# Softmax attention's logits and values as fp32r passes over four heads

## The chip, the core and the metric

The kernel runs on one core of one Trainium2 chip. A core has five engines with their own instruction queues: TensorE (PE in the profile; its weight loads have a row of their own, PEld), VectorE (DVE), ScalarE (ACT), GpSimd (POOL) and SyncE (SP), which here only issues DMAs. Matrix products land in PSUM, eight banks of 128 partitions x 512 f32; everything else lies in SBUF, 128 partitions wide. The metric is the device time of one execution in microseconds, as the median of several runs.

## The reference

One decoder layer in f32: a SwiGLU network, a pair of token mixers side by side, a second SwiGLU network, each behind a modulated RMSNorm, for 256 positions of width 2048. What matters here is the second mixer, sliding-window attention with 32 query heads, 8 key and value heads (four query heads share one) of width 64, blocks of 128 positions and one sink per query head:

```python
def swa_with_sinks(q, k, v, sinks):
    ...
    kb, vb = band(k), band(v)          # the block before, and the own block
    logits = jnp.einsum('bnqhgd,bnkhd->bnhgqk', qb, kb).astype(jnp.float32) * (d ** -0.5)
    ...
    logits = jnp.where(valid[None, :, None, None], logits, NEG_INF)
    sink = ...
    probs = jax.nn.softmax(jnp.concatenate([logits, sink], axis=-1), axis=-1)[..., :-1]
    out = jnp.einsum('bnhgqk,bnkhd->bnqhgd', probs.astype(v.dtype), vb)
    return out.reshape(b, s, hq * d)
```

With 256 positions there are two blocks (t = 0 and 1 below). The first block sees its own 128 keys, the second its own and those of the first.

## The kernel before, in words

Every large product (`products`, L322 to L324) is made of three fp32r passes. The weight and the activation are each split into a rounded part, `hi`, cast by ScalarE, and the rest, `lo`, which VectorE gets by subtraction; hi*hi, hi*lo and lo*hi are added in PSUM. A projection of 512 output columns, here called a chunk, takes 96 such passes into two PSUM banks (`pa`, four in all, so that chunk n+2 needs the banks of chunk n emptied). The weight is loaded in quarters of a chunk (`load`, L307), each split in two halves (`wh` by L330, `wl` by L331) into a pool of three.

The token mixers' stage runs the chunks of one projection: keys and values of the softmax attention, four chunks of its queries, two of the retention's queries (called rq here) and two of its keys (rk), four of its values (rv), then gates. The attention's own work runs beside the later chunks: `window(pair)` is a Python generator for two query heads, and `step()` takes one piece of it after each quarter chunk. VectorE has further side work in this stage, a matrix-vector product for the conditioning (L203).

For a pair of heads, `window_weights` makes the logits with plain f32 matmuls (L959 for the first block, L962 for the second). The transposed keys `skt` exist twice, with the other half of the partitions zeroed, so that 128 partitions of two query heads can be multiplied with either. Then come scale and mask (L965), maximum (L975, L976), exponential (L996), sum and scaling (L1005), all in one pair tile `a` (a pool of two). `window_values` transposes the weights (L440 into `pd`, a pool of two banks), copies them out (L441 into `t`, a pool of five tiles of 128 x 512) and makes f32 matmuls with the values (L1024, L1028, L1031), whose result is copied into `qo` (L1034). A query chunk is copied out of PSUM into two `t` tiles (L1053) and transposed into `qo`; an rq or rk chunk goes through the rotary (L1074, L1080, L1085, L1086), also with `t` tiles, two for each bank.

The order of SyncE's queue is the program's. Those of PE, VectorE and ScalarE come from a scheduler that, when the program is built, follows the program's order but lets an instruction whose operands and buffers are ready pass one that waits. Once built, every engine's order is fixed.

Of the kernel before, what the change touches and what calls it, by code (L numbers as in the profile page):

```python
# [16 lines left out]
P = 128  # L17
# [25 lines left out]
def constants():  # L43
# [12 lines left out]
    for h in range(RH):  # L56
# [8 lines left out]
                sin.transpose(1, 0, 2).reshape(P, -1),  # L65
                causal,
                before,
# [9 lines left out]
def layer_kernel(  # L77
# [822 lines left out]
    dec = one.tile([P, D], F32, tag="row", name="dec")  # L900
    nc.gpsimd.dma_start(dec, consts[:, C_DEC:])
# [12 lines left out]
    for t in range(NT):  # L914
        nc.gpsimd.dma_start(x_d[:, t, :], x_sb[:, t, :])
    skt = one.tile([P, NT, D], F32, tag="x", name="skt").rearrange(
        "p i (h s) -> p i h s", h=KVH
    )
    VW = HD + KVH * P
    b = in_chunk(O_SV, ready)  # L920
    for t in range(NT):
        for g in range(2):
            kd = t512()
            nc.vector.tensor_copy(
                kd.rearrange("p (h a d) -> p h a d", h=4, a=2),
                head[t][:, g * 256 : (g + 1) * 256]
                .rearrange("p (h d) -> p h d", h=4)[:, :, None, :]
                .broadcast_to([P, 4, 2, HD]),
            )
            ps = bank()  # L930
            for j in range(4):
                js = slice(j * P, (j + 1) * P)
                nc.tensor.transpose(ps[:, js], kd[:, js], ident)
            for i in range(2):
                hs = slice(i * HD, (i + 1) * HD)
                nc.any.tensor_copy(
                    skt[hs, i, g * 4 : g * 4 + 4, t * P : (t + 1) * P],
                    ps[hs].rearrange("p (h s) -> p h s", h=4),
                )
    nc.vector.memset(skt[HD:, 0], 0.0)  # L940
    nc.vector.memset(skt[:HD, 1], 0.0)
    sv = slot()[:, : NT * VW].rearrange("p (t n) -> p t n", t=NT)
    nc.vector.memset(sv, 0.0)
    for t in range(NT):
        nc.any.tensor_copy(
            sv[:, t, HD:].rearrange("p (h d) -> p h d", h=KVH)[:, :, :HD],
            b[t].rearrange("p (h d) -> p h d", h=KVH),
        )
    qo = slot().rearrange("p (k s) -> p k s", s=S)

    mask = small_c[:, C_MASK : C_MASK + 3 * P]

    def window_weights(pair):

        kv = pair // 2
        lg = pair_tile()[:, :, : 3 * P]
        for i in range(2):
            ps = side_bank()
            nc.tensor.matmul(  # L959
                ps[:, :P], qo[:, pair, :P], skt[:, i, kv, :P], start=True, stop=True  # L960
            )
            nc.tensor.matmul(  # L962
                ps[:, P : 3 * P], qo[:, pair, P:], skt[:, i, kv, :], start=True, stop=True
            )
# [7 lines left out]
            )  # L972
        mx = small(4, "mx")
        m2 = mx.rearrange("p (t i) -> p t i", t=2)
        nc.vector.tensor_reduce(out=m2[:, 0, :], in_=lg[:, :, :P], axis=AX.X, op=ALU.max)  # L975
        nc.vector.tensor_reduce(out=m2[:, 1, :], in_=lg[:, :, P:], axis=AX.X, op=ALU.max)  # L976
        sb = sink_b[:, 2 * pair : 2 * pair + 2]
# [14 lines left out]
        for t in range(2):  # L992
            for i in range(2):
                seg = lg[:, i, :P] if t == 0 else lg[:, i, P:]
# [6 lines left out]
        for t in range(2):  # L1001
            for i in range(2):
                seg = lg[:, i, :P] if t == 0 else lg[:, i, P:]
# [4 lines left out]
        return lg  # L1008

    def window_values(pair, lg):  # L1010

        kv = pair // 2
        prs = []
        for i in range(2):
            pr = a512()
            transpose_to(
                pr[:, : 3 * P], lambda j: lg[:, i, j * P : (j + 1) * P], 3, side_bank()
            )
            prs.append(pr)
        po = side_bank()  # L1020
        for i, pr in enumerate(prs):
            vs = slice(kv * P + (1 - i) * HD, kv * P + (1 - i) * HD + P)
            first, last = i == 0, i == 1
            nc.tensor.matmul(po[:, :P], sv[:, 0, vs], pr[:, :P], start=first, stop=last)  # L1024
        for i, pr in enumerate(prs):
            vs = slice(kv * P + (1 - i) * HD, kv * P + (1 - i) * HD + P)
            first, last = i == 0, i == 1
            nc.tensor.matmul(  # L1028
                po[:, P:S], sv[:, 0, vs], pr[:, P : 2 * P], start=first, stop=False
            )  # L1030
            nc.tensor.matmul(  # L1031
                po[:, P:S], sv[:, 1, vs], pr[:, 2 * P : 3 * P], start=False, stop=last
            )
        nc.any.tensor_copy(qo[:, pair, :], po[:, :S])  # L1034

    before = []

    def window(pair):
        lg = window_weights(pair)
        yield  # L1040
        if before:
            window_values(*before.pop())
        before.append((pair, lg))
        if pair == QH // 2 - 1:
            yield
            window_values(*before.pop())
        yield

    for ci in range(4):
        b = in_chunk(O_SQ + ci * CH)  # L1050
        for t in range(NT):
            u = t512()
            nc.any.tensor_copy(u, b[t])  # L1053
            transpose_to(
                qo[:, ci * 4 : ci * 4 + 4, t * P : (t + 1) * P],
                lambda j: u[:, j * P : (j + 1) * P],
                4,
            )
        side += [window(pair) for pair in range(ci * 4, ci * 4 + 4)]
# [33 lines left out]

    vo = slot().rearrange("p (t n) -> p t n", t=NT)
# [194 lines left out]
```

## Time and profile before

| | |
|---|---|
| median of 3 runs | 2455.85 us (2454.01 to 2459.7) |
| the profiled execution's own time | 2457.51 us |
| its span | 2455.7 us |
| PE busy | 2410.4 us, 98% |
| DVE busy | 1706.5 us, 69% |
| ACT busy | 1192.9 us, 49% |
| mean granted PE clock | 0.996 |

The span runs from the first to the last instruction; what the execution takes beside it is 1.8 us. Busy time is the time in which an engine has at least one instruction under way. A recorded duration includes the way out of the engine's pipeline, during which the next instruction may already run; so what an instruction takes from its engine is read from one start to the next, and how late its result is from its duration. In a group's row the columns are line, engine, operation, tiles out<-in, shapes and count, then busy time, mean duration in ns, and the engine's idle time before them with what ended it.

### The profile page before, as it was taken

The numbers are of one execution on the slowest core, as the hardware profiler recorded it, in microseconds if no ns is written. First come the engines' busy times: TensorE is split into PE (matmuls) and PEld (weight loads), VectorE is DVE, ScalarE is ACT, GpSimd is POOL, SyncE is SP. The second block draws the span as 40 slices with busy tenths as digits, with TensorE's granted clock in tenths as the row PEclk, the third lists the DMA queues.
The fourth block names the chain that finished last, engine by engine and source line by source line (L and its number), as shares of the span: only waits on it lengthen the run. The fifth ranks groups of instructions, "written<-read, shape, count | busy, mean of one in ns | idle before, by whom it ended". The sixth has DMA issues, their size and how long they took to land.

```text
span 2455.7 us, 29144 instructions
## 1 busy us (share of the span) xinstructions
PE 2410.4 (98%) x10910; PEld 1985.3 (81%) x10910; DVE 1706.5 (69%) x2731; ACT 1192.9 (49%) x1623; POOL 7.7 (0%) x18
## 2 busy tenths in 40 slices
PE   7999999999999999999999999999999999999998
PEld 5778888887787888888888788887888888888886
DVE  7898877777877677886666776767655555545656
ACT  6544544444546554455544454446544444444544
POOL 0000000000000000000000000000000000000000
PEclk9999999999999999999999999999999999999999
DMA  9997687888876665556676777855566666665563
GB/s 357 340 332 271 234 313 296 326 303 297 311 254 228 231 228 195 205 190 239 230 278 240 258 260 257 276 188 187 206 223 234 228 223 225 238 223 192 188 202 120
DMA packets 244657, 603.27 MB, mean 246 GB/s; under 512 B 9698, under 2 KB 10082, under 8 KB 225186
## 3 DMA queue, kind: packets, MB, share of 16 engines
q1 hardware_dynamic: 243010, 591.61, 67.8%
q0 software_dynamic: 1504, 9.81, 1.0%
q8 instruction: 85, 1.39, 0.2%
q14 instruction: 58, 0.47, 0.1%
HBM read 597.16 MB, written 4.22 MB: 245 GB/s over the span
## 4 chain that ended last, share of the span: by engine, by line
PE 89%; DVE 4%; DMA 1%; ACT 1%; issue 1%; SPq 0%; DVEq 0%; ACTq 0%
PE pa L324 28%; PE pa L323 28%; PE pa L322 28%; PE ps L440 1%; DVE wl L331 1%; DVE slot L203 1%; DMA slot<-in_w_ada_dram 1%; PE pd L962 1%; PE pd L440 0%; DVE home L429 0%; DVE slot L863 0%; PE pd L1024 0%; PE pd L1028 0%; PE pd L1031 0%; PE pd L959 0%
## 5 line engine op out<-in xcount | busy, mean ns | idle before, releaser
L331 DVE TENSOR_TENSOR wl<-raw,wh 128x1024 fp32r<-128x1024 f32 (+1 forms) x788 | 947.6, 1207 | 582.0 <-ACT wh L330 580.2
L330 ACT CAST wh<-raw 128x1024 fp32r<-128x1024 f32 (+1 forms) x788 | 819.5, 1041 | 1043.7 <-PE pa L323 1021.4
L322 PE MATMUL pa<-wh,hh 128*128 128x512 f32 x2200 | 862.4, 393 | 2.2 <-ACT wh L330 1.7
L323 PE MATMUL pa<-wh,hl 128*128 128x512 f32 x2200 | 861.8, 392 | 1.8 <-DVE hl L500 1.8
L324 PE MATMUL pa<-wl,hh 128*128 128x512 f32 x2200 | 796.8, 393 | 2.3 <-DVE wl L331 2.2
L322 PEld LDWEIGHTS pa<-wh,hh 128*128 128x128 f32 x2200 | 413.4, 188 | 89.4 <-ACT wh L330 2.4
L323 PEld LDWEIGHTS pa<-wh,hl 128*128 128x128 f32 x2200 | 413.8, 188 | 87.8 <-DVE hl L500 2.5
L324 PEld LDWEIGHTS pa<-wl,hh 128*128 128x128 f32 x2200 | 410.9, 188 | 89.4 <-DVE wl L331 6.5
L323 PE MATMUL pa<-wh,a 128*128 128x512 f32 x992 | 384.3, 390 | 1.3 <-DVE a L363 1.3
L324 PE MATMUL pa<-wl,a 128*128 128x512 f32 x992 | 368.1, 391 | 1.3 <-DVE wl L331 1.3
L322 PE MATMUL pa<-wh,a 128*128 128x512 f32 x992 | 367.7, 391 | 1.0 <-ACT wh L330 0.5
L324 PEld LDWEIGHTS pa<-wl,a 128*128 128x128 f32 x992 | 185.9, 188 | 42.4 <-DVE wl L331 4.1
L322 PEld LDWEIGHTS pa<-wh,a 128*128 128x128 f32 x992 | 186.6, 188 | 41.4 <-DVE t L552 1.4
L323 PEld LDWEIGHTS pa<-wh,a 128*128 128x128 f32 x992 | 186.5, 188 | 40.3 <-DVE a L363 1.7
L203 DVE CUSTOM_DVE_ANT_0 slot<-slot,cact 128x512 f32<-128x512 f32 (+1 forms) x252 | 192.9, 815 | 28.7 <-DMA slot<-in_w_ada_dram 28.2
L203 DVE CUSTOM_DVE_ANT_0 raw<-raw,cact 128x512 f32<-128x512 f32 (+1 forms) x260 | 166.7, 696 | 43.2 <-DMA raw<-in_w_ada_dram 33.7
L363 DVE TENSOR_TENSOR a<-slot,a 128x512 fp32r<-128x512 f32 x124 | 84.9, 685 | 3.8 <-ACT a L362 3.8
L362 ACT CAST a<-slot 128x512 fp32r<-128x512 f32 x124 | 76.4, 618 | 5.3 <-PE pa L324 5.2
L441 ACT COPY slot<-ps 128x512 f32<-128x512 f32 x76 | 42.4, 586 | 34.8 <-PE ps L440 34.3
L429 DVE TENSOR_TENSOR wl<-raw,wh 128x1024 fp32r<-128x1024 f32 x34 | 41.4, 1223 | 17.4 <-ACT wh L426 17.1
L426 ACT CAST wh<-raw 128x1024 fp32r<-128x1024 f32 x34 | 35.3, 1050 | 17.4 <-PE pa L323 17.3
L203 DVE DVE_READ_ACCUMULATOR2_ANT sums<- 128x1 f32 x512 | 42.5, 83 | 0.0
(171 smaller groups left out, 1174.2 us busy)
## 6 DMA issues: line engine op xcount, KB each, us to landing
raw<-in_w_ffn_gu_dram SPq DMA_DIRECT2D x152, 1024.0 KB, 4.9
raw<-in_w_in_dram SPq DMA_DIRECT2D x104, 1024.0 KB, 5.0
raw<-in_w_ffn_down_dram SPq DMA_DIRECT2D x88, 1024.0 KB, 5.2
slot<-in_w_ada_dram SPq DMA_DIRECT2D x76, 1024.0 KB, 7.6
raw<-in_w_ada_dram SPq DMA_DIRECT2D x64, 1024.0 KB, 4.9
raw<-in_w_ffn_gu_dram SPq DMA_DIRECT2D x24, 768.0 KB, 7.0
raw<-in_w_swa_branch_dram SPq DMA_DIRECT2D x16, 1024.0 KB, 5.2
raw<-in_w_ret_branch_dram SPq DMA_DIRECT2D x16, 1024.0 KB, 5.3
```

The costliest lines, as they stand in the source:

```text
L203: nc.vector.tensor_tensor_reduce(out=w[:, at], in0=w[:, at], in1=cact[:, at], scale=1.0, scalar=0.0, op0=ALU.mult, op1=ALU.add, accum_out= ...
L322: nc.tensor.matmul(ps, ah[:, j, ts], wh[:, j, :], start=first, stop=False)
L323: nc.tensor.matmul(ps, al[:, j, ts], wh[:, j, :], start=False, stop=False)
L324: nc.tensor.matmul(ps, ah[:, j, ts], wl[:, j, :], start=False, stop=last)
L330: nc.scalar.copy(hi, src)
L331: nc.vector.tensor_sub(lo, src, hi.bitcast(F32))
L362: nc.scalar.copy(hi, v)
L363: nc.vector.tensor_sub(lo, v, hi.bitcast(F32))
L426: nc.scalar.copy(self.hi, self.src)
L429: nc.vector.tensor_sub(self.lo, self.src, self.hi.bitcast(F32))
L440: nc.tensor.transpose(ps[:, j * P : (j + 1) * P], src_of(j), ident)
L441: nc.any.tensor_copy(dest, ps[:, : n * P])
```

## The change

Query, key, probability and value are split like the weights. The query's rounded part lies on one half of the partitions and its rest on the other; the keys stand on both halves, once rounded (`keys[:, 0]`) and once as rest (`keys[:, 1]`). So one pass gives (hi + lo) times the keys' rounded part and a second adds (hi + lo) times their rest. Each pass covers 256 key positions; for the first block 128 of them are not used. The value side puts the value's rounded part and rest side by side as the stationary operand (64 + 64 columns), and takes four heads' transposed probabilities, 512 wide, as the moving one, first their rounded part, then their rest. The upper and the lower half of the result are then added (L1043, L1047). A generator now covers one key head, four query heads: two steps of weights, then the turn and the values. Both tiles of the pool `a` hold that key head's logits until they are transposed. The load of the retention's `dec` moves behind the attention, as its place holds two heads' queries.

```diff
-                causal,
-                before,
+                before,
                 causal,
+                causal,
...
-    skt = one.tile([P, NT, D], F32, tag="x", name="skt").rearrange(
+    keys = one.tile([P, 2, KVH, S], F32R, tag="x", name="keys")
...
+            hi, lo = (
+                keys[:, i, g * 4 : g * 4 + 4, t * P : (t + 1) * P] for i in range(2)
+            )
+            p4 = ps.rearrange("p (h s) -> p h s", h=4)
+            nc.scalar.copy(hi, p4)
+            nc.vector.tensor_sub(lo, p4, hi.bitcast(F32))
...
-    nc.vector.memset(skt[HD:, 0], 0.0)
-    nc.vector.memset(skt[:HD, 1], 0.0)
-    nc.vector.memset(sv, 0.0)
...
+        nc.scalar.copy(sv[:, t, :, 0, :], v8)
+        nc.vector.tensor_sub(sv[:, t, :, 1, :], v8, sv[:, t, :, 0, :].bitcast(F32))
...
-            nc.tensor.matmul(
-                ps[:, :P], qo[:, pair, :P], skt[:, i, kv, :P], start=True, stop=True
-            )
-            nc.tensor.matmul(
-                ps[:, P : 3 * P], qo[:, pair, P:], skt[:, i, kv, :], start=True, stop=True
-            )
+            qs = query(kv)[:, 2 * pairs + i, :]
+            for t, at in ((1, slice(0, S)), (0, slice(S, 2 * S))):
+                for n in range(2):
+                    nc.tensor.matmul(
+                        ps[:, at],
+                        qs[:, t * P : (t + 1) * P],
+                        keys[:, n, kv, : at.stop - at.start],
+                        start=n == 0,
+                        stop=n == 1,
+                    )
...
+    def window_turn(lgs):
+
+        for z in range(3):
+            ps = side_bank()
+            for i in range(4):
+                nc.tensor.transpose(
+                    ps[:, i * P : (i + 1) * P],
+                    lgs[i // 2][:, i % 2, z * P : (z + 1) * P],
+                    ident,
+                )
+            nc.scalar.copy(wh3[:, z, :], ps)
+            nc.vector.tensor_sub(wl3[:, z, :], ps, wh3[:, z, :].bitcast(F32))
+
+    def window_values(kv):
+
+        for t, zs in ((0, ((0, 2),)), (1, ((0, 0), (1, 1)))):
+            po = side_bank()
+            for kt, z in zs:
+                st = sv[:, kt, kv].rearrange("p i d -> p (i d)")
+                nc.tensor.matmul(po, st, wh3[:, z, :], start=z != 1, stop=False)
+                nc.tensor.matmul(po, st, wl3[:, z, :], start=False, stop=z != 0)
+            y = t512()
+            nc.scalar.copy(y, po)
+            p4, y4 = (v.rearrange("p (j a s) -> p j a s", j=2, a=2) for v in (po, y))
+            for a in range(2):
+                here, there = (slice(c * HD, (c + 1) * HD) for c in (a, 1 - a))
+                nc.vector.tensor_add(
+                    qo[here, 2 * kv : 2 * kv + 2, t * P : (t + 1) * P],
+                    p4[there, :, a, :],
+                    y4[here, :, a, :],
+                )
+
+    def window(kv):
+        lgs = []
+        for pairs in range(2):
+            window_weights(kv, pairs, lgs)
+            yield
         yield
+        window_turn(lgs)
+        window_values(kv)
...
+            for j in range(2):
+                q4 = query(2 * ci + j).rearrange("p (j a) s -> p j a s", a=2)
+                p2 = ps[:, j * S : (j + 1) * S].rearrange("p (j s) -> p j s", j=2)
+                for a in range(2):
+                    here, there = (slice(c * HD, (c + 1) * HD) for c in (a, 1 - a))
+                    hi = q4[here, :, a, t * P : (t + 1) * P]
+                    nc.scalar.copy(hi, p2[here])
+                    nc.vector.tensor_sub(
+                        q4[there, :, a, t * P : (t + 1) * P], p2[here], hi.bitcast(F32)
+                    )
+        side += [window(kv) for kv in (2 * ci, 2 * ci + 1)]
```

In the changed kernel's lines L968 is the logit pass, L975 scale and mask, L987 the maximum, L1008 the exponential, L1017 the scaling, L1026 the transposes, L1031 and L1032 cast and subtraction, L1040 and L1041 the value passes, L1043 and L1047 the values' copy and additions, L1066 a query chunk's copy, L1077 and L1078 the query's split, L1096 to L1108 the rotary.

The orders below are those of the built programs. First, PE before, in the first rk chunk: the three transposes of one head's weights (`pd_7802`), the values' first matmul of the other head, whose copy `t_7795` is older, and then products of the chunk (`pa_7841`, `pa_7842`).

```order
L322 MATMUL pa_7842<-wh_8031,hh_4118 128x512
L440 MATMUL pd_7802<-small_c,a_7608 128x128 x3
L1024 MATMUL pd_7807<-t_7795,slot_6364 128x128
L323 MATMUL pa_7842<-wh_8031,hl_4119 128x512
L324 MATMUL pa_7842<-wl_8032,hh_4118 128x512
L322 MATMUL pa_7841<-wh_8048,hh_4118 128x512
L323 MATMUL pa_7841<-wh_8048,hl_4119 128x512
L324 MATMUL pa_7841<-wl_8049,hh_4118 128x512
```

The second matmul of the values follows 14 products later. After, PE at the end of the second rk chunk (`pa_8386`), for key head 6: transposes into three banks (`pd_8185`, `pd_8192`, `pd_8199`), value passes into two, the next head's first logits, and only then the next chunk's products (`pa_8599`). Rows that occur twice are left out.

```order
L324 MATMUL pa_8386<-wl_8554,hh_4118 128x512
L1026 MATMUL pd_8185<-small_c,a_8051 128x128
L1026 MATMUL pd_8192<-small_c,a_8051 128x128
...
L1026 MATMUL pd_8199<-small_c,a_7980 128x128 x2
L1026 MATMUL pd_8199<-small_c,a_8051 128x128 x2
L1040 MATMUL pd_8206<-wt_6366,spare_6360 128x512
L1041 MATMUL pd_8206<-wt_6366,spare_6360 128x512
L1040 MATMUL pd_8213<-wt_6366,spare_6360 128x512
L1041 MATMUL pd_8213<-wt_6366,spare_6360 128x512
...
L968 MATMUL pd_8223<-keys,more 128x256 x4
L322 MATMUL pa_8599<-wh_8603,hh_4118 128x512
```

Transposes, values and logits now stand next to one another, without products between them. The same run ends the chunks before it. PE at the end of the second rq chunk: key head 3's last value pass, the four heads' logits of key head 4, and then already the transposes of their weights (`a_7529`).

```order
L1041 MATMUL pd_7520<-wt_6366,spare_6360 128x512
L968 MATMUL pd_7530<-keys,spare_6360 128x256 x4
L968 MATMUL pd_7536<-keys,spare_6360 128x256 x4
L968 MATMUL pd_7601<-keys,spare_6360 128x256 x4
L968 MATMUL pd_7607<-keys,spare_6360 128x256 x4
L1026 MATMUL pd_7704<-small_c,a_7529 128x128
L1026 MATMUL pd_7711<-small_c,a_7529 128x128
```

Here a whole key head passes through PE with no product in between. At the same place VectorE has the subtractions of key head 4's transposed weights, the additions of its values, and among them the rotary of the first rq chunk, whose banks (`pa_7455`, `pa_7456`) the first rk chunk needs.

```order
L1032 TENSOR_TENSOR wt_6366<-pd_7711,wt_6366 128x512
L1032 TENSOR_TENSOR wt_6366<-pd_7718,wt_6366 128x512
L1047 TENSOR_TENSOR slot_6365<-pd_7725,t_7728 64x2x128 x2
L1096 TENSOR_TENSOR t_7774<-pa_7455,small_c 128x512
L1102 TENSOR_TENSOR t_7775<-pa_7455,small_c 128x4x64 x2
L1096 TENSOR_TENSOR t_7787<-pa_7456,small_c 128x512
L1102 TENSOR_TENSOR t_7788<-pa_7456,small_c 128x4x64 x2
L1047 TENSOR_TENSOR slot_6365<-pd_7732,t_7737 64x2x128 x2
```

The emptying of a chunk's banks now stands behind the additions of a key head that the program places ahead of it.

More of the change, by code (lines that the diff above doesn't have):

```diff
@@ L949, in layer_kernel, with query @@
     qo = slot().rearrange("p (k s) -> p k s", s=S)
+    wt = slots.tile([P, KD * S], F32R, tag="slot", name=nm("wt"))
+    wh3, wl3 = (
+        wt[:, i * 3 * CH : (i + 1) * 3 * CH].rearrange("p (z n) -> p z n", n=CH)
+        for i in range(2)
+    )
+    more = one.tile([P, D], F32R, tag="row", name="more")
+    cells = [t[:, n * 4 * S : (n + 1) * 4 * S] for t, n in (
+        (spare, 2), (spare, 3), (wt, 3), (more, 0), (spare, 2), (spare, 3), (wt, 3), (more, 1)
+    )]
+    def query(kv):
+        return cells[kv].rearrange("p (i s) -> p i s", s=S)
@@ L951, in layer_kernel, with window_weights @@
     mask = small_c[:, C_MASK : C_MASK + 3 * P]
-    def window_weights(pair):
-        kv = pair // 2
+    def window_weights(kv, pairs, lgs):
+        sb = sink_b[:, 4 * kv + 2 * pairs : 4 * kv + 2 * pairs + 2]
         lg = pair_tile()[:, :, : 3 * P]
+        lgs.append(lg)
         for i in range(2):
             ps = side_bank()
-            nc.tensor.matmul(
-                ps[:, :P], qo[:, pair, :P], skt[:, i, kv, :P], start=True, stop=True
-            )
-            nc.tensor.matmul(
-                ps[:, P : 3 * P], qo[:, pair, P:], skt[:, i, kv, :], start=True, stop=True
-            )
+            qs = query(kv)[:, 2 * pairs + i, :]
[8 more added lines that the diff above has]
+                    )
@@ L972, in window_weights @@
             )
+        segs = (slice(S, 3 * P), slice(0, S))
         mx = small(4, "mx")
         m2 = mx.rearrange("p (t i) -> p t i", t=2)
-        nc.vector.tensor_reduce(out=m2[:, 0, :], in_=lg[:, :, :P], axis=AX.X, op=ALU.max)
-        nc.vector.tensor_reduce(out=m2[:, 1, :], in_=lg[:, :, P:], axis=AX.X, op=ALU.max)
-        sb = sink_b[:, 2 * pair : 2 * pair + 2]
+        for t in range(NT):
+            nc.vector.tensor_reduce(
+                out=m2[:, t, :], in_=lg[:, :, segs[t]], axis=AX.X, op=ALU.max
+            )
         nc.vector.tensor_tensor(
@@ L991, in window_weights @@
         sm = small(4, "sm")
-        for t in range(2):
+        for t in range(NT):
             for i in range(2):
-                seg = lg[:, i, :P] if t == 0 else lg[:, i, P:]
+                seg = lg[:, i, segs[t]]
                 z = 2 * t + i
@@ L1000, in window_weights @@
         nc.vector.reciprocal(sm, sm)
-        for t in range(2):
+        for t in range(NT):
             for i in range(2):
-                seg = lg[:, i, :P] if t == 0 else lg[:, i, P:]
+                seg = lg[:, i, segs[t]]
                 z = 2 * t + i
@@ L1007, in window_weights @@
                 )
[L1008 to L1034, printed above, removed]
@@ new lines, in window_values @@
+    def window_values(kv):
[14 more added lines that the diff above has]
+                    y4[here, :, a, :],
+                )
@@ L1053, in layer_kernel @@
             nc.any.tensor_copy(u, b[t])
[L1054 to L1059, printed above, removed]
+            ps = bank()
+            for j in range(4):
+                js = slice(j * P, (j + 1) * P)
+                nc.tensor.transpose(ps[:, js], u[:, js], ident)
+            for j in range(2):
[7 more added lines that the diff above has]
+                        q4[there, :, a, t * P : (t + 1) * P], p2[here], hi.bitcast(F32)
+                    )
+        side += [window(kv) for kv in (2 * ci, 2 * ci + 1)]
     qk = slot().rearrange("p (a h s) -> p a h s", a=2, h=RH)
@@ L1091, in layer_kernel @@
                 )
+    dec = one.tile([P, D], F32, tag="row", name="dec")
+    nc.gpsimd.dma_start(dec, consts[:, C_DEC:])
     vo = slot().rearrange("p (t n) -> p t n", t=NT)
```

27 lines of the change are left out of this document (3 added, 24 removed).

## The prediction

> **What bounds the kernel now.** I read the page first: busy shares, then the chain of waits.
>
> ```profile
> PE 2410.4 (98%) x10910; PEld 1985.3 (81%) x10910; DVE 1706.5 (69%) x2731; ACT 1192.9 (49%) x1623; POOL 7.7 (0%) x18
> ...
> PE 89%; DVE 4%; DMA 1%; ACT 1%; issue 1%; SPq 0%; DVEq 0%; ACTq 0%
> ```
>
> TensorE (PE) is on the ending chain for 89% of the span. Then busy time by stretch: 855 to 1078 us holds the projection chunks under which softmax attention runs (columns: PE, weight load, VectorE, ScalarE, GpSimd, clock, DMA share).
>
> ```profile
> 855.00:1078.00 223.00, 221.76 (x1143) 187.30 (x1142) 170.31 (x373) 113.05 (x239) 0.00 (x0) 1.00 0.60 208
> ```
>
> PE is busy throughout. VectorE (DVE) is at 76%. So PE work removed here shortens the kernel if, and only if, PE keeps finding work. Next, PE's timeline, for true costs: the recorded duration of a matmul includes a tail that overlaps the next, so I go from start to start.
>
> ```profile
> 886.46 0.39 PE L322 MATMUL pa<-wh,hh 128*128 128x512 f32 x1
> 886.69 0.38 PE L1024 MATMUL pd<-t,slot 128*128 128x128 f32 x2
> 886.91 0.39 PE L1028 MATMUL pd<-t,slot 128*128 128x128 f32 x2
> 887.13 0.39 PE L1031 MATMUL pd<-t,slot 128*128 128x128 f32 x2
> ...
> 887.80 0.60 PE L440 MATMUL ps<-small_c,t 128*128 128x128 f32 x4
> 888.24 0.39 PE L959 MATMUL pd<-skt,slot 128*128 128x128 f32 x2
> 888.46 0.60 PE L962 MATMUL pd<-skt,slot 128*128 128x256 f32 x2
> 888.71 0.58 PE L323 MATMUL pa<-wh,hl 128*128 128x512 f32 x1
> 889.13 0.40 PE L324 MATMUL pa<-wl,hh 128*128 128x512 f32 x1
> ```
>
> A 512-wide fp32r product takes 0.23 us (886.46 to 886.69). An f32 matmul is recorded twice: 128 wide it takes 0.22 us (886.91 to 887.13); 256 wide 0.44 (888.46 to 889.13 is 0.67, less one product). A transpose takes 0.11 (four from 887.80 to 888.24).
>
> **The change, part by part: PE work.** Before, a pair of heads has two logit matmuls per head (0.22 + 0.44) and six value matmuls (0.22): 2 x 0.66 + 6 x 2 x 0.11 = 2.65 us, and 16 pairs make 42.3. After, a key head (four query heads, eight in all) has 16 logit passes 256 wide and 6 value passes 512 wide. No row shows a 256-wide fp32r pass. Its cost lies between half a 512-wide product (0.114) and a whole one (0.228); I take half, since the f32 rows scale with width. That is 1.82 + 1.37 = 3.19 us, 25.5 in all. Transposes stay (12 per four heads; query and keys too). PE loses **16.8 us**; with the dear pass 2.2.
>
> **What takes their place on DVE and ScalarE (ACT).** Groups of this stage, by shape (count, busy us, mean ns of one):
>
> ```profile
> L996 ACT ACTIVATE a<-a,ng 128x256 f32<-128x256 f32 x32 | 15.8, 496 | 0.0
> ...
> L996 ACT ACTIVATE a<-a,ng 128x128 f32<-128x128 f32 x32 | 12.6, 396 | 0.3 <-DVE ng L982 0.2
> ...
> L441 ACT COPY slot<-ps 128x512 f32<-128x512 f32 x18 | 10.3, 585 | 10.3 <-PE ps L440 10.2
> ```
>
> and DVE's timeline, for start to start:
>
> ```profile
> 883.60 1.01 DVE L1005 TENSOR_SCALAR a<-a,sm 128x128 f32<-128x128 f32 x4
> ...
> 982.33 1.23 DVE L331 TENSOR_TENSOR wl<-raw,wh 128x1024 fp32r<-128x1024 f32 x1 [0.33 <-ACT wh L330]
> 983.47 0.55 DVE L965 SCALAR_TENSOR_TENSOR a<-pd,small_c 128x384 f32<-128x384 f32 x1
> 984.05 0.42 DVE L975 TENSOR_REDUCE mx<-a 128x2 f32<-128x256 f32 x1
> 984.39 0.68 DVE L976 TENSOR_REDUCE mx<-a 128x2 f32<-128x512 f32 x1
> 985.10 0.16 DVE L978 TENSOR_TENSOR mx<-mx,sink_b 128x4 f32<-128x4 f32 x1
> ...
> 988.03 0.69 DVE L1074 TENSOR_TENSOR t<-pa,small_c 128x512 f32<-128x512 f32 x1
> 988.63 0.42 DVE L1080 TENSOR_TENSOR t<-pa,small_c 128x256 f32<-128x256 f32 x1
> 988.97 0.17 DVE L1000 RECIPROCAL sm<-sm 128x4 f32<-128x4 f32 x1
> ```
>
> A 512-wide operation on a PSUM bank occupies DVE 0.60 us (988.03 to 988.63) and hands on its result after 0.68; a 256-wide one 0.34 (988.63 to 988.97) and 0.42. Per key head DVE gains three 512-wide subtractions (L1032) and four 256-wide additions (L1047): 3.2 us, 25 in all; the query's 32 subtractions (L1078) add 11. DVE then has 170 + 36 = 206 us of work in a stage whose PE time would be 223 - 17 = 206. The three memsets that go lie ahead of this stretch and save nothing here.
>
> **Where PE comes to wait.** Today the probabilities' transposes are followed by products, which cover the copy out of PSUM. The one place where the order leaves a gap shows what that costs:
>
> ```profile
> 1047.83 0.49 PE L440 MATMUL pd<-small_c,a 128*128 128x128 f32 x3
> ...
> 1048.16 0.39 PE L1024 MATMUL pd<-t,slot 128*128 128x128 f32 x2
> 1048.36 0.56 DVE L441 COPY t<-pd 128x384 f32<-128x384 f32 x1 [0.68 <-PE pd L440]
> ...
> 1048.97 0.49 PE L1024 MATMUL pd<-t,slot 128*128 128x128 f32 x2 [0.43 <-DVE t L441]
> ```
>
> PE stands from 1048.38 to 1048.97, 0.6 us, for one copy. In the changed order every key head but the fourth ends on a run of PE rows without a product: transposes into two banks, the third bank's transposes (which wait until the first bank is cast and subtracted), value passes (which wait for the third cast and subtraction), the next head's first logits (whose bank waits for copy and additions). I add it up from T0, the start of the last transposes: first bank done 0.49, cast 1.1 (ACT 0.585), subtraction 1.9 (DVE 0.68), third bank's transposes 2.0 to 2.6, cast 3.2, subtraction 3.9; value passes from 3.3, the last starting at 4.9; the first value bank copied 5.0, added 5.9; logits 5.9 to 6.4. Products resume at 6.5, for their banks are emptied (L1066) behind those additions. PE worked 2.7 of the 6.5: it stands 3.8. Where the weight cast ahead of these casts on ACT must itself wait for PE's last product, 0.6 more; for the first key head, whose third transposes are still covered by products, 3.0. Bounds 3 and 5; I take 4, six times: **+24**. For key heads 5 to 7 the bank is emptied by the rotary's rows (L1096, L1102: 0.60 + 2 x 0.34 = 1.3 before the first bank is free, 2.5 for both): **+4** (0 to 7.5).
>
> The double one: at the end of the second rq chunk stand key head 3's end, the whole of key head 4 and head 5's first logits, without a product. Both pair tiles hold a key head until it is transposed, so head 4 can start only there. Its chain from its first logits (5.9 after T0): four scale-and-mask operations (L975, 0.55 each, through two banks), reductions (0.34 + 0.71), small rows of 0.2 us each: the exponentials' bias is there at 11.3; four exponentials a pair and a small one, about 1.85 us (2 x 0.40 + 2 x 0.50 and the rest): 13.2 and 15.0; sum and reciprocal, 1.0 for four scalings: 16.6; then the single chain again, 22.4, and 1.3 of rotary: 23.7, of which PE works 7. **+17**; with better overlap of the two pairs 10, at worst 20.
>
> The query's split writes one tile with ACT and DVE in turn, each waiting for the other: four rounds of about 0.37 + 0.42 instead of 1.4 us of DVE time. Products cover most of it: **+2** (0 to 5). PE's present waits here, 0.4 and 0.8 us on L1024, go: **-1**.
>
> **The clock.** At the norm ahead of this stage PE had a stretch like these islands: its longest idle piece, then two stretches with their granted clock (third number from the end).
>
> ```profile
> 780.26 0.80 PE L323 MATMUL pa<-home,hl 128*128 128x512 f32 x1 [1.59 <-DVE hl L545]
> ```
>
> ```profile
> 776.00:780.30 4.30, 2.71 (x15) 1.65 (x12) 1.83 (x5) 2.93 (x7) 0.00 (x0) 1.00 0.35 138
> 780.30:783.80 3.50, 3.50 (x9) 2.82 (x10) 2.86 (x10) 2.00 (x7) 2.66 (x5) 0.51 0.37 108
> ```
>
> PE was 63% busy for 4.3 us, and the next 3.5 us ran at 0.51. An island is 41% busy for 6.5 us, so each may be followed by 3.4 us at half clock: 1.7 us lost, seven times 12. Some of that falls where PE waits anyway: **+8** (0 to 12). [...] The trace halves the clock after a longest idle piece of 1.6 us, so I keep the row.
>
> Sum: -16.8 + 24 + 4 + 17 + 2 + 8 - 1 = **+37 us**. The profiled execution took 2457.51 us (span 2455.7), 1.7 above the median of the runs; 2494.5 there, **2493** against the median.
>
> **Rivals.**
> (a) PE's saving comes through: the islands are covered, because casts and subtractions are ready early. For: today's waits are 1.2 us in all, and PE was on the chain for 89%. Against: no product stands in those rows to cover them. 2455.9 - 16.8 = 2439. It decides if PE stands under 2 us a key head.
> (b) It cancels: 2 us per head and a double island of 5 or less: about 2456.
> (c) DVE also runs short between islands: it has 206 us of work, and idles 53 now (223 - 170). If some 20 us of that idling stays outside the islands, weight rests (L331) come late as well: 2513. For: the equality of both loads. Against: the islands lengthen the stage and give DVE room.
> (d) The 256-wide pass is as dear as a 512-wide one: the change doesn't shorten PE work as it says, +14.6: 2508. Against: f32 rows scale with width.
>
> **How the numbers follow.** Forecast 0.62, (a) 0.11, (b) 0.09, (c) 0.13, (d) 0.05. The forecast's own bounds: -16.8 + 18 + 10 - 1 = +10 and -16.8 + 30 + 7.5 + 20 + 5 + 12 = +58, 2466 to 2514. To hold 8 in 10 with (b) partly and (c): 2456 to 2518. A difference under 0.2% (5 us) can't be told from none: faster 0.12, same 0.08, slower 0.80.
>
> **What would show it.** After: PE waits on the transposes L1026 (for L1032) and on the value passes L1040 and L1041 (for L1031 and L1032), each about 1 us, eight times, and one wait of 4 us or more on L1026 for the scaling L1017; half-clock stretches of 3.4 us between 880 and 1130; L968 passes 0.11 apart. It would be wrong if L1026, L1040 and L1041 wait less than 15 us together, or if PE's waits stand at L324 for L331 (rival c).

## The result, and the profile after

The changed kernel takes 2501.07 us (median of 4 runs, 2497.74 to 2502.94), the kernel before 2454.93: a ratio of 1.0181, 95% interval [1.0166, 1.0196], slower. The prediction was 2493 us, in a range of 2456 to 2518. The profiled execution took 2501.36 us (before: 2457.51), so there are 43.9 us to account for.

The head of the page of the changed kernel, and the row of granted clocks in 40 slices:

```profile
span 2499.6 us, 28978 instructions
...
PE 2418.1 (97%) x10766; PEld 1979.1 (79%) x10766; DVE 1743.8 (70%) x2820; ACT 1203.2 (48%) x1637; POOL 7.7 (0%) x18
...
PEclk9999999999999999799999999999999999999999
```

PE is busy for 8 us more than before although it has less to do, and one slice, 1000 to 1062 us, shows a clock of 0.7. Next the waits of PE between 780 and 1300 us (the waiting row, what it waited for, us in total, how often, the longest); before, 1.2 us stood here in the attention's rows:

```profile
PE pd L1026 <- DVE wt L1032: 12.4, 7, 2.5
PE pd L1026 <- DVE a L1017: 9.6, 4, 5.6
PE pd L1040 <- ACT wt L1031: 5.4, 7, 1.1
PE pd L1041 <- DVE wt L1032: 2.9, 5, 1.0
PE pd L968 <- DVE slot L1047: 2.4, 2, 1.5
PE pa L323 <- DVE hl L545: 1.6, 1, 1.6
PE pa L322 <- ACT t L1066: 1.2, 1, 1.2
PE pd L1040 <- DVE wt L1032: 1.0, 1, 1.0
```

But for the norm's L323 all of it is new: 34.9 us, on transposes, value passes, logits, and one chunk's start. On L324 PE waits once, 0.2 us, for the rest of a weight that is kept in place (L429), and never for L331. An island is a run of PE rows without a product between them, as in the prediction; the double one, in the timeline of PE (start, length, line, shapes, count, and in brackets the idle time ahead and its releaser):

```profile
997.31 0.39 PE L324 MATMUL pa<-wl,hh 128*128 128x512 f32 x1
997.54 0.60 PE L1026 MATMUL pd<-small_c,a 128*128 128x128 f32 x4
1000.59 0.66 PE L1026 MATMUL pd<-small_c,a 128*128 128x128 f32 x4 [2.45 <-DVE wt L1032]
1001.92 0.80 PE L1040 MATMUL pd<-wt,spare 128*128 128x512 f32 x1 [0.68 <-ACT wt L1031]
1002.65 0.80 PE L1041 MATMUL pd<-wt,spare 128*128 128x512 f32 x1
...
1006.81 2.10 PE L968 MATMUL pd<-keys,spare 128*128 128x256 f32 x12 [0.91 <-DVE slot L1047]
1014.48 1.09 PE L1026 MATMUL pd<-small_c,a 128*128 128x128 f32 x4 [5.56 <-DVE a L1017]
1016.23 1.11 PE L1026 MATMUL pd<-small_c,a 128*128 128x128 f32 x4 [0.67 <-DVE a L1017]
1018.59 1.12 PE L1026 MATMUL pd<-small_c,a 128*128 128x128 f32 x4 [1.24 <-DVE wt L1032]
1020.43 0.80 PE L1040 MATMUL pd<-wt,spare 128*128 128x512 f32 x1 [0.73 <-ACT wt L1031]
...
1024.91 0.80 PE L322 MATMUL pa<-wh,hh 128*128 128x512 f32 x1
```

The last product ahead starts at 997.31, the next at 1024.91: 27.6 us in which PE serves only one key head's end and a whole second one. The same transposes that last 0.60 at 997.54 last 1.09 at 1014.48: the granted clock is 0.50 there (1012.19 to 1015.60). Between the products on either side the six single islands measure 5.8, 9.1, 9.9, 12.8, 9.2 and 9.0 us.

**Where the 43.9 us are.** Both kernels make the same products in the same order, so the n-th product of one is set against the n-th of the other. Between the 3264th (806.1 us before) and the 4656th (1203.7 before) every matmul is entered at its price at full clock, read from start to start in the two profiles (0.227 for 512 columns, 0.115 for an fp32r pass of 256, 0.218 and 0.109 for the records of a plain 256 and 128); what a slow record takes above it, up to the double, is put down to the clock, and longer gaps to waiting.

| us | before | after | difference |
|---|---|---|---|
| products | 316.0 | 316.0 | 0 |
| other matmuls | 76.7 | 60.5 | -16.2 |
| PE waits | 1.6 | 46.1 | +44.5 |
| half clock on PE's rows | 0 | 14.5 | +14.5 |
| not resolved | 3.2 | 3.2 | 0 |
| sum | 397.5 | 440.3 | +42.7 |

(The waits come out higher here than in the view because the view counts a matmul's whole recorded duration, 0.27 us for a transpose that holds PE for 0.11, as busy. How a slow row that stands ahead of a wait is entered moves 1 to 2 us between the two rows: by the granted clock alone they are 43.7 and 16.0.) The changed kernel was 1.2 us ahead where this stretch begins, and loses 2.3 behind it, most of it near 1403 us, where PE waits 2.7 us for a split (L363) instead of 1.3 and two half-clock stretches follow (6.83 us) instead of one (3.41); with these it is 43.9. The runs below differ from the kernel before at that place by -2.4 to +3.6 us, so these 2.3 are not put down to the attention.

### The profile page after: what moved, and what is told of

Its sections match the earlier page's. It is cut to its first block, busy times and chain, and to the rows that moved or that the text cites. A ratio compares the mean times of both kernels' runs of the same rounds, so it can differ in the third digit from the quotient of the medians.

```text
span 2499.6 us, 28978 instructions
## 1 busy us (share of the span) xinstructions
PE 2418.1 (97%) x10766; PEld 1979.1 (79%) x10766; DVE 1743.8 (70%) x2820; ACT 1203.2 (48%) x1637; POOL 7.7 (0%) x18
## 4 chain that ended last, share of the span: by engine, by line
PE 86%; DVE 5%; ACT 2%; DMA 1%; issue 1%; DVEq 0%; SPq 0%; ACTq 0%
PE pa L323 28%; PE pa L324 27%; PE pa L322 27%; DVE wl L331 1%; PE ps L440 1%; DVE slot L203 1%; PE pd L968 1%; DMA raw<-in_w_ada_dram 0%; ACT wh L330 0%; DVE home L429 0%; DVE slot L863 0%; PE pd L1026 0%; PE pd L1041 0%; DMA slot<-in_w_ada_dram 0%; DVE raw L203 0%
## 5 line engine op out<-in xcount | busy, mean ns | idle before, releaser
L331 DVE TENSOR_TENSOR wl<-raw,wh 128x1024 fp32r<-128x1024 f32 (+1 forms) x788 | 948.1, 1208 | 571.3 <-ACT wh L330 567.6
L323 PE MATMUL pa<-wh,hl 128*128 128x512 f32 x2200 | 859.9, 391 | 1.9 <-DVE hl L500 1.9
L324 PE MATMUL pa<-wl,hh 128*128 128x512 f32 x2200 | 790.5, 393 | 2.3 <-DVE wl L331 2.2
L323 PEld LDWEIGHTS pa<-wh,hl 128*128 128x128 f32 x2200 | 414.6, 188 | 87.9 <-DVE hl L500 2.6
L324 PEld LDWEIGHTS pa<-wl,hh 128*128 128x128 f32 x2200 | 411.4, 188 | 89.8 <-DVE wl L331 6.2
L323 PE MATMUL pa<-wh,a 128*128 128x512 f32 x992 | 385.1, 391 | 2.7 <-DVE a L363 2.7
L324 PE MATMUL pa<-wl,a 128*128 128x512 f32 x992 | 368.4, 391 | 1.1 <-DVE wl L331 1.1
L323 PEld LDWEIGHTS pa<-wh,a 128*128 128x128 f32 x992 | 187.1, 189 | 42.3 <-DVE a L363 3.6
L324 PEld LDWEIGHTS pa<-wl,a 128*128 128x128 f32 x992 | 186.2, 188 | 41.8 <-DVE wl L331 3.6
L363 DVE TENSOR_TENSOR a<-slot,a 128x512 fp32r<-128x512 f32 x124 | 85.0, 686 | 3.8 <-ACT a L362 3.8
L429 DVE TENSOR_TENSOR wl<-raw,wh 128x1024 fp32r<-128x1024 f32 x34 | 41.4, 1224 | 17.4 <-ACT wh L426 17.1
L441 ACT COPY slot<-ps 128x512 f32<-128x512 f32 x67 | 37.1, 587 | 27.0 <-PE ps L440 26.6
```

The lines of the kernel that those rows point to most:

```text
L323: nc.tensor.matmul(ps, al[:, j, ts], wh[:, j, :], start=False, stop=False)
L324: nc.tensor.matmul(ps, ah[:, j, ts], wl[:, j, :], start=False, stop=last)
L331: nc.vector.tensor_sub(lo, src, hi.bitcast(F32))
L363: nc.vector.tensor_sub(lo, v, hi.bitcast(F32))
L429: nc.vector.tensor_sub(self.lo, self.src, self.hi.bitcast(F32))
L441: nc.any.tensor_copy(dest, ps[:, : n * P])
```

## The experiments

All times are medians, over four to ten executions (two for the turn by pairs that is not overlapped); ratios are to the kernel before on the same chip, which took 2453.75 to 2455.72 us. Every edit also gives the engines newly built orders, so a microsecond or two of a single run is not the price of its edit alone.

| run | us | ratio, 95% interval |
|---|---|---|
| logits alone | 2451.67 | 0.9986 [0.9977, 0.9995] |
| values alone | 2494.49 | 1.0158 [1.0143, 1.0173] |
| turn by pairs, overlapped | 2468.43 | 1.0054 [1.0037, 1.0071] |
| turn by pairs, not overlapped | 2541.51 | 1.0349 [1.0330, 1.0368] |
| change without the copy's tile | 2491.67 | 1.0146 [1.0131, 1.0161] |
| turn by pairs, values in the keys' place | 2460.38 | 1.0020 [1.0011, 1.0029] |
| the same with two more banks | 2449.87 | 0.9977 [0.9965, 0.9989] |
| the same, scaling on ScalarE | 2442.91 | 0.9957 [0.9943, 0.9970] |
| the same, half the scaling on ScalarE | 2438.66 | 0.9938 [0.9925, 0.9952] |
| scaling on ScalarE, no copy's tile | 2440.88 | 0.9945 [0.9931, 0.9958] |
| change with half the scaling on ScalarE | 2493.65 | 1.0161 [1.0142, 1.0181] |
| change with 96 more passes | 2509.49 | 1.0217 [1.0201, 1.0233] |

The theory: PE waits because transposes, casts, value passes and the next logits of one key head stand in a row without a product, and they do so because one key head holds both pair tiles. The rivals: VectorE has too much work; the added steps cost their latency wherever they stand; the ring of five `t` tiles holds up the emptying of a chunk's banks.

### Each half alone

Logits alone: the kernel before with the split keys and queries.

```diff
...
-                ps[:, :P], qo[:, pair, :P], skt[:, i, kv, :P], start=True, stop=True
...
+                        ps[:, at], qs[:, t * P : (t + 1) * P],
+                        keys[:, n, kv, : at.stop - at.start], start=n == 0, stop=n == 1,
...
```

> The kernel before with the change's logits alone (keys and queries split, 128 passes of 256 columns); values as before, pair by pair, in plain f32. My theory (PE's waits come from the value side: three casts and subtractions in a row, and both pair tiles held by one key head): PE work for the logits falls from 20.9 to 14.6 us, the query's split is covered, waits stay under 4 us, so 2455 - 6 + 2 = 2451 (2447 to 2456). Rival 'work of VectorE' (32 subtractions for the queries, 11 us, and the 3 us for the keys are what PE waits for): 2460 or more, with waits on the weights' rests. If the 256-wide pass cost as much as a 512-wide one: 29 us of logits, 2463.

Values alone: the changed kernel with the plain f32 logits.

```diff
...
-                        keys[:, n, kv, : at.stop - at.start],
...
+                ps[:, :S], qo[:, pair, P:], skt[:, i, kv, :], start=True, stop=True
...
```

> The changed kernel with the logits of before (plain f32 from the unsplit queries and the doubled keys, whose halves are zeroed), four heads turned and multiplied together as in the change. My theory: the islands stay: 30 to 40 us of PE waits on the transposes and value passes and some 10 us at half clock, less 10 us of PE work in the values: 2490 (2480 to 2500). Rival 'work of VectorE': without the query's subtractions most of the loss is gone, 2465 or less.

2451.67 and 2494.49: the logits gain 3 to 4 us, the values lose 39. So the narrow passes are not dear, and the bulk of the waits comes without the query's 32 subtractions, which the second of these kernels doesn't have. But the halves don't add up: 4 gained and 39 lost would make 35, and together they lose 46. In the stretch of the table the change has 6 us less work for PE than the values alone and still takes 1.7 us longer; its first island, 897 to 903 us, is not there with the values alone, and the double one is 27.6 us long instead of 25.6. So beside the values the logits' side, its splits included, adds some 8 us of standing and slow clock; which of its rows do it, no run here shows. The waits of PE with the values alone are those of the change (L1018 the transposes, L1024 the subtraction, L1009 the scaling, L1032 the value pass, L1023 the cast there):

```profile
PE pd L1018 <- DVE wt L1024: 10.3, 5, 2.4
PE pd L1018 <- DVE a L1009: 6.3, 3, 5.4
PE pd L1032 <- ACT wt L1023: 5.6, 7, 1.0
```

### The ring of copy tiles

```diff
-            y = t512()
-            nc.scalar.copy(y, po)
...
+                out = qo[here, 2 * kv : 2 * kv + 2, t * P : (t + 1) * P]
+                nc.scalar.copy(out, p4[here, :, a, :])
+                nc.vector.tensor_add(out, out, p4[there, :, a, :])
```

> The changed kernel, but the value product's one half is copied straight to its place in the output and the other half added there, so that the 16 copies take no tile of the ring of five, behind which a chunk's evacuation stands. Rival 'ring' (the products are missing at the chunk's end because their banks are emptied behind the value copies): the waits go, 2465 or less. My theory (the chain of one key head at a time sets the pace, about 30 us each, and the ring only decides where PE meets it): the early islands go, but the heads that are not done stand in one row of 134 PE rows without a product before the retention's values may be stored: 30 to 40 us of waits there, 2485 to 2505.

2491.67, as the theory had it. Product by product this kernel gains all the way and loses it at one place: the 4272nd product (1093.9 us before) comes 32.7 us earlier than before, the 4320th (1107.7 before) 40.3 us later. The ring does decide where PE meets the work that is left over, and without it the products run further ahead; but the windows keep their pace of one key head at a time, and what is left of them stands in one row ahead of the retention's values, which need the slot that the attention's values hold. Its waits:

```profile
PE pd L1026 <- DVE a L1017: 23.9, 8, 6.6
PE pd L1026 <- DVE wt L1032: 4.9, 4, 1.2
```

### Overlapping two pairs

The same passes, but a pair is turned alone (`finish`, with the values behind a key head's second pair), after the next pair's logits, with two casts a pair, one of 512 and one of 256 columns:

```diff
-        window_turn(lgs)
-        window_values(kv)
...
             window_weights(kv, pairs, lgs)
             yield
+            if before:
+                finish(*before.pop())
+            before.append((kv, pairs, lgs[0]))
...
+        for zs in ((0, 1), (2,)):
```

> The changed kernel with the same casts, subtractions and passes, but the turn made for each pair as soon as the next pair's logits are issued, so that a pair tile is free after its own six groups of transposes and two pairs overlap as before the change. Per key head four casts and subtractions (two of 512, two of 256 columns) instead of three of 512: VectorE's work is the same within 1 us. My theory (a key head holds both tiles until its turn, so nothing overlaps): the islands go but for the last key head's (34 rows without a product, some 10 us of waits): 2455 - 17 + 10 + 2 for the rest and 3 for the clock = 2453 (2446 to 2462). Rival 'the steps themselves' (casts and subtractions between PE's rows cost their latency wherever they stand): 8 heads x 4 steps x 1 us, 2480 or more. Rival 'work of VectorE': 2490 to 2500, as the change.

And with the turn right behind each pair's own weights, ahead of the next pair's logits:

```diff
             window_weights(kv, pairs, lgs)
             yield
+            window_turn(lgs[0], pairs)
+        window_values(kv)
```

> The turn by pairs with the same instructions, but in the program each pair's turn stands right behind its own weights, ahead of the next pair's logits, and a key head has two steps instead of four. If the overlap of two pairs is what helped: long rows without a product come back (62, 54 and 50 PE rows), 2490 or more. If the smaller pieces helped (a pair tile free after six transposes, four short casts): 2475 or less.

2468.43 and 2541.51, with the same instructions but for two, which go from VectorE to ScalarE. Of the change's loss of 46 us to the kernel before, 33 go with the overlapped turn; without the overlap, small pieces make things worse than the change. The waits, first overlapped (L1027 the transposes, L1037 the subtraction, L1045 the value pass, L1052 the additions, L1118 the rotary), then not:

```profile
PE pd L968 <- DVE slot L1052: 8.5, 4, 3.7
PE pd L1027 <- DVE a L1017: 5.6, 1, 5.6
PE pa L322 <- DVE t L1118: 2.6, 1, 2.6
PE pd L1045 <- DVE wt L1037: 1.8, 2, 1.2
```

```profile
PE pd L1027 <- DVE a L1017: 62.1, 11, 9.3
PE pd L968 <- DVE slot L1052: 4.0, 3, 2.1
PE pd L1045 <- DVE wt L1037: 2.9, 8, 0.8
```

In the second, eleven times a whole softmax (scale and mask to scaling) passes while PE stands, 5.6 us on average. It also takes half as many steps for each key head, so the two runs differ in pace as well as in order. In the first the waits for casts and subtractions are nearly gone (1.8 us above, and 0.7 on the value pass behind it): here, with products between them, the steps cost little. I had expected 2453 (2446 to 2462), so this missed. The 4272nd product is 0.9 us ahead of the kernel before, the 4320th 14.9 behind: the last key head costs 15.8 us, of which I had expected 10. And ahead of it little of the saved PE work shows yet; four waits for the additions, of up to 3.7 us, were not expected at all: the next logits need a bank that the additions still read.

### The last key head, and the banks

First the retention's values in the keys' place, then the logits in the banks of the projections' transposes as well.

```diff
-    vo = slot().rearrange("p (t n) -> p t n", t=NT)
+    vo = one.tile([P, NT, D], F32, tag="x", name="vo")
```

> The turn by pairs, and the retention's values take the place of the attention's keys instead of that of its values, so that they wait for the last logits and not for the last value passes. In the turn by pairs 24 us were lost in the row of PE rows without a product before the retention's values (34 rows); now this row has 20. My theory (the work still open when the place is needed is done without cover): some 10 to 15 us come back, 2468 - 12 = 2456 (2449 to 2462). Rival 'the steps cost their latency wherever they stand': the same rows wait a little later, 2465 to 2470.

```diff
-            ps = side_bank()
+            ps = bank()
```

> The run before, and the logits in the two banks of the projections' transposes instead of the two shared with turn and values, so that the next pair's logits don't wait until the additions have read the value banks. The longest row without a product has 14 PE rows (20 in the run before, 52 in the change). My theory: PE's waits fall under 6 us, the clock stays up, and the saving of 17 us in PE work shows: 2455 - 17 + 4 = 2442 (2436 to 2449), faster than the kernel before. Rival 'work of VectorE' (36 us more than before in the same stretch): with PE's work gone VectorE sets the pace, 2452 or more, waits on the weights' rests.

2460.38: at the 4368th product 14.4 us of the turn by pairs' loss are gone (1.8 behind instead of 16.2), 8 in the median. 2449.87 with the banks, faster than before, but 1 us outside what I expected. PE's waits are then:

```profile
PE pd L1027 <- DVE slot L1052: 3.3, 1, 3.3
PE pa L324 <- DVE wl L331: 2.7, 1, 2.7
...
PE pa L322 <- DVE t L1118: 0.9, 1, 0.9
```

One of 2.7 us is now for a weight's rest; in the run before it was 0.4. In this kernel VectorE is busy for 244.84 of 270 us, PE for 263.04 (the columns are span, then busy time of PE, weight loads, VectorE, ScalarE and GpSimd, then clock and DMA):

```profile
850.00:1120.00 270.00, 263.04 (x1279) 219.07 (x1278) 244.84 (x548) 155.04 (x321) 0.53 (x1) 0.99 0.63 218
```

### VectorE's load

The scaling of the weights on ScalarE, all of it or, in two of the four runs, only where `t` is 1; the third run adds the edit on the copy's tile, the fourth is the change itself with half the scaling moved.

```diff
-                nc.vector.tensor_scalar(
-                    out=seg, in0=seg, scalar1=sm[:, z : z + 1], scalar2=None, op0=ALU.mult
-                )
+                nc.scalar.mul(seg, seg, sm[:, z : z + 1])
```

> The turn by pairs with the two more banks, and the 64 scalings of the weights moved from VectorE (16.1 us there) to ScalarE. With the two more banks VectorE is busy for 255 of 285 us and PE waits 2.7 us for a weight rest and 3.3 us for value additions. My theory (VectorE is the next bound once the islands are gone): 3 to 6 us come back, 2446 (2441 to 2449). If VectorE's load costs nothing there: 2450, no change. If ScalarE, which makes the casts, now comes late: 2453 or more.

> Only the second block's 32 scalings (those of 256 columns) on ScalarE. By the same theory 2447 (2443 to 2450), between the run without and the run with all of them on ScalarE; 2450 if the load of VectorE costs nothing.

> All scalings on ScalarE, and the value copies without tiles of the ring. If the ring still held up a chunk's evacuation, 2 to 3 us less than with the scalings alone; by my theory (with two pairs overlapping the windows keep up, and the ring no longer matters) the same within 3 us, 2446.

> The changed kernel as it is, and only the second block's 32 scalings on ScalarE, the edit that took 11 us off the turn by pairs. My theory (in the change PE waits for a key head's chain, in which VectorE is mostly free): the long rows without a product stay (52 and six of 10 to 22 PE rows), the double island is shorter by one scaling's difference or two, 2497 (2490 to 2503). Rival 'work of VectorE' (it is the load of VectorE that makes PE wait in the change too): 10 us less as there, or more, 2490 or less.

2442.91, 2438.66 and 2440.88, whose intervals overlap, so which share of the scaling is best isn't settled. The second missed: I had expected 2447 (2443 to 2450), between none of the scaling moved and all of it, and it lies below that range. So whether VectorE's load explains all of the gain stays open. The ring, which would have shown as 2 to 3 us between the first and the third, can't be told from nothing. With half of the scaling moved PE has 1.4 us of waits between 780 and 1300 us and is busy for 268.65 of 270 us at a clock of 1.00:

```profile
PE pa L324 <- DVE wl L331: 1.2, 2, 0.8
PE pa L324 <- DVE home L429: 0.2, 1, 0.2
```

```profile
850.00:1120.00 270.00, 268.65 (x1320) 224.42 (x1319) 243.33 (x529) 171.97 (x361) 0.54 (x1) 1.00 0.65 226
```

In the change itself the same edit takes off 7.4 us by the medians (2493.65) and 5 by the ratios, whose intervals just overlap. That is less than the 11.2 of the turn by pairs (10 by the ratios) and not down to the 2490 of the rival, and it leaves the rows and their waits: 35.7 us in the view against 34.9. So VectorE's load is not the bulk of what PE waits for in the change; that it became the next limit when the islands were gone is likely by the weight's rest that PE waited for and by the gain, but not shown further. The two profiled runs are 9.0 us apart. Of these 5.2 lie in the stretch of the table, where thirteen half-clock stretches stand instead of fifteen (mean clock 0.988 against 0.986), and the rest lies behind it, near 1403 us in the change, outside the attention.

Turn by pairs, keys' place, two more banks and half the scaling together make a version that beats both kernels: 0.62% under the one before, 2.5% under the change.

### Work for the waiting PE

```diff
             nc.vector.tensor_sub(wl3[:, z, :], ps, wh3[:, z, :].bitcast(F32))
+            junk = bank()
+            for _ in range(4):
+                nc.tensor.matmul(junk, keys[:, 0, 0, :P], wh3[:, z, :], start=True, stop=True)
```

> The changed kernel with 96 passes of 128x512 more, whose results nobody reads: four behind each cast of turned weights, reading that cast, in the rows where PE waits. They are 21.8 us of PE work. If PE's waits are as long as the trace says (about 1 us for each of 24 subtractions) and the clock halves because PE waits: most of the passes fit into waits, some 10 us stand on the path, and of the 13 us that half clock costs some 8 come back: 2503 (2494 to 2510), mean granted clock 0.991 or more. Rival 'the clock doesn't go by PE's waits': clock 0.986 as in the change, 2510 or more. If PE did not wait in these rows, all 22 us are added: 2523.

2509.49, mean clock 0.991: within the expected range, at its upper end. 21.8 us of passes cost 8.4 by the medians. In the stretch of the table the profiled run is 12.6 us longer than the change's, so there some 9 us of the passes cost nothing: entered by the granted clock, the waits fall by 4.5 us (43.7 to 39.2) and the slow clock by 5.2 (16.0 to 10.8), with nine half-clock stretches instead of fifteen. From 850 to 1135 us the granted clock is 0.96, in the change 0.91. So with passes in the waits less of this run went by at half clock; that the waits hold the greater part of the passes is not shown.

## Why the prediction was right, point by point

**The saving in PE work**, predicted -16.8, is -16.2. The narrow passes are cheap, as the rows of plain f32 had suggested: at full clock neighbouring ones of one tile start 0.115 to 0.119 us apart (1007.01, 1007.12, 1007.24), not 0.228. Rival (d) is out. The saving is worked out from counts and these prices; that it is real shows in the turn by pairs with half the scaling moved, which ends 15 us under the kernel before.

**The islands.** Six single ones with their rotary were to cost 24 + 4 = 28 us of standing, and cost 28.9 (3.6, 4.1, 5.8 for key heads 0 to 2; 7.0, 4.1, 4.3 for 5 to 7). The double one was to cost 17, and cost 14.9. The query's split (+2) and today's waits (-1) are not told apart from these. All in all 24 + 4 + 17 + 2 - 1 = 46 was predicted and 44.5 measured. The rotary's share was put too high: key heads 5 to 7 stand 1.9 us longer in all than 0 to 2, not 4. So the islands' mechanism was right, but that the total came out within 2 us is partly luck: the single islands without the rotary were put too low (4 each, and key heads 0 to 2 cost 4.5 on average), the rotary and the double island too high. The sign for being wrong, under 15 us of waits on L1026, L1040 and L1041, is far off: they are 31.3 in the view. The single wait of the scaling, "4 us or more", is 5.6. The wait of the third transposes for the subtraction was to be about 1 us and is 1.8 on average. The timeline of VectorE, ScalarE and PE at the start of the double island shows why:

```profile
997.23 2.58 DVE L331 TENSOR_TENSOR wl<-raw,wh 128x1024 fp32r<-128x1024 f32 x2
997.51 1.05 ACT L330 CAST wh<-raw 128x1024 fp32r<-128x1024 f32 x1 [1.61 <-PE pa L323]
997.54 0.60 PE L1026 MATMUL pd<-small_c,a 128*128 128x128 f32 x4
998.58 1.07 ACT L1031 CAST wt<-pd 128x512 fp32r<-128x512 f32 x2
999.85 1.29 DVE L1032 TENSOR_TENSOR wt<-pd,wt 128x512 fp32r<-128x512 f32 x2
```

The cast of the turned weights stands behind the cast of the next chunk's weights, which itself waited until PE's last product (L323) had left its buffer, and the subtraction behind two weight rests. I had named that cast as a possible 0.6 us more; the weight rests beside it I had not. The island at 928 us shows the same rows, the one at 1087 the cast and one weight rest.

**The clock is the step that was mis-sized:** +8 (0 to 12) predicted, 14.5 measured, outside its bounds. I had put one half-clock stretch of 3.4 us behind each island, seven in all, with a third of their cost on waiting. There were fifteen, none at the first island and up to five at the double one, and most of their time lies inside the islands. The last section sets them beside PE's busy time. The row that the term was taken from, one such stretch behind a wait of 1.59 us, was short of that. With 14.5 in place of 8 the sum would have been 43.7. The stretch of the table, where all its terms lie, measured 42.7; by the medians the loss is 46.1.

**The rivals.** (a) and (b) would have needed under 2 us a key head: it is 4.8. (c), VectorE short between the islands: no wait on L324 for L331 in the change, and less work for VectorE left its waits as they were. But that I counted the two loads as equal (206 and 206) was a fair warning: once the islands were gone, PE did wait for a weight's rest.

**What the prediction left open** is why the rows stand alone. It described the order; it did not say which part of the program makes it so. The runs do: the ring of `t` tiles only chooses the place, that one key head's chain overlaps no other makes the windows slow, and the shared banks and the slot for the retention's values add to it. That a key head holds both pair tiles is not the whole reason: the run that is not overlapped needs one tile for a pair, and is slower still, with fewer steps. So what counts is the order in which the program places a turn and the next pair's logits, as far as two runs show that also differ in pace.

## What to carry to other kernels

When side work runs in the shadow of a matmul stream, count how many of its chains can be under way at once, not only its busy time: here eight key heads one after another cost PE 59 us of waits and slow clock, for 16 us less work; two pairs overlapping took off 33 of the loss of 46 at once, and more banks, an earlier free place and half a scaling moved brought the 16 us out. Look in the built order for rows without a product, and price them start to start; add what the clock takes, here 14.5 us beside 44.5 of waits. And when a saving fails to show, take away the waits one after the other, since the next limit (banks, then VectorE) only appears when the one before it has gone.

## What the runs showed of the hardware

What follows is measured on one run, the profiled one of the changed kernel, whose trace records the granted clock. The seven slow pieces of its attention last 3.41, 6.83, 10.24 or 13.65 us, one to four times 3.413, and each begins a whole number of times 3.413 after the one before. In stretches of that length (span, PE's busy time and count, clock, DMA):

```profile
899.56:902.97 3.41, 1.80 (x6) 1.00 0.59 250
902.97:906.38 3.41, 2.98 (x13) 1.00 0.15 11
...
960.99:964.40 3.41, 1.70 (x9) 1.00 1.05 375
964.40:967.81 3.41, 1.90 (x8) 0.99 0.47 197
967.82:971.23 3.41, 1.93 (x6) 0.50 0.18 20
...
998.53:1001.94 3.41, 0.67 (x5) 0.99 0.93 306
1001.95:1005.36 3.41, 3.41 (x7) 0.51 0.27 105
1005.36:1008.77 3.41, 2.38 (x16) 1.00 0.00 0
1008.77:1012.18 3.41, 0.14 (x2) 0.99 0.00 0
1012.19:1015.60 3.41, 1.09 (x4) 0.50 0.00 0
1015.60:1019.01 3.41, 1.54 (x6) 0.50 0.00 0
1019.01:1022.42 3.41, 2.68 (x8) 0.50 0.00 0
1022.42:1025.84 3.42, 3.32 (x9) 0.51 0.00 0
1025.84:1029.25 3.41, 3.41 (x16) 1.00 0.00 0
```

Of these stretches at full clock, the ones with 1.80 and 1.70 us busy were followed by full clock (1.00 and 0.99), those with 0.67 and 0.14 by half (0.51 and 0.50), but the one with 1.90 also by half (0.50): in this run recorded busy time alone doesn't decide. In the double island the half-clock stretch with 2.68 us busy was followed by another (0.51), the one with 3.32 by full clock (1.00). The stretch ahead of that island's first fall was not idle: 0.67 us of work were in it. So the clock fell inside an island and rows that remained in it ran at about half speed (0.43 us from pass to pass, below); in the double island four stretches on end had a clock of 0.50 or 0.51, with 1.09, 1.54, 2.68 and 3.32 us busy. That PE's waits between the rows kept the clock down there is my reading. The run with 96 more passes fits it, with a mean clock of 0.991 instead of 0.986, but no run shows it by itself.

A second thing: in the stretch at 0.51 from 1001.95 the fp32r passes of 512 columns start 0.43 us apart (1003.24, 1003.67, 1004.10), at full clock 0.227 (996.63, 996.86, 997.08, 997.31), which is more than half of it. What the remaining 0.014 us are, no run here shows.
